# A partial product put off by one chunk, and its bank's copy split in two, in a matrix product with RMS norm

## The chip, the cores and the metric

One core of a Trainium2 chip. The metric is the device time of one execution in microseconds (us); lower is better. Engines: PE is TensorE's matmul, PEld its weight load, DVE is VectorE, ACT is ScalarE, POOL is GpSimd (which here issues most loads), SP is SyncE.

## The reference

```python
a, b = randn(2048, 2048), randn(2048, 2048)      # float32; gamma: randn(2048); eps = 1e-5
x = np.matmul(a, b)
rms = np.sqrt(np.mean(x ** 2, axis=-1, keepdims=True) + eps)
return (gamma * x / rms).astype(np.float32)
```

## The kernel before

Only the head of the kernel, its first 40 us, is touched. There the first four blocks of 128 rows of A are multiplied with the left half of B while both still arrive. The contraction of 2048 is cut into eight chunks `kp` of two contraction tiles `kt` (128 each).

Each chunk is three loads: one slice of A, 4 x 128 rows by 256 columns, and two tiles of B, each 128 x 1024. They are cast from float32 to bf16 on the way.

```python
    def load_head(kp):
        nc.gpsimd.dma_start(
            out=ah(kp),
            in_=a[0:HB * P, kp * W2:(kp + 1) * W2].rearrange("(r p) k -> p r k", p=P))
        load_b(0, kp)                      # two dma_starts, one per contraction tile
```

The slice of A is transposed on TensorE, eight transposes into the one PSUM bank `tbank`, and VectorE copies it out:

```python
    def transpose_head(kp):
        bank = ps_t.tile([P, CH], FP32, name="tbank")        # pool ps_t has one buffer
        ...                                                  # 8 transposes of ah(kp), line 168
        nc.vector.tensor_copy(out=head_at[:, 2 * kp:2 * kp + 2, :, :], in_=view)   # line 173
```

Seven of the eight output groups (4 row blocks x 2 column halves) have a bank of their own and accumulate over all chunks (line 388). The eighth has none. It is computed as a partial product per chunk, also in `tbank` (line 419), and added up in SBUF:

```python
    def stream_in_parts(g, kp):
        part = ps_t.tile([P, CH], FP32, name="tbank")
        for t in range(2):
            nc.tensor.matmul(part, head_at[:, 2 * kp + t, g[0], :], head_rhs(g[1], 2 * kp + t),
                             start=(t == 0), stop=(t == 1))
        x = x_chunk(*g)
        if kp == 0:
            nc.scalar.copy(out=x, in_=part)
        else:
            nc.vector.tensor_tensor(out=x, in0=part, in1=x, op=ALU.add)
    ...
    for kp in range(KP):
        ...                                                  # loads of chunk kp + 4
        before = [lambda: transpose_head(kp + 1)] if kp + 1 < KP else []
        ...
        stream(groups1, kp, before, len(groups1) + (5 if kp == 0 else 3))
        ...
        stream_in_parts(last1, kp)
```

In chunks 0 to 6 `stream` issues the 14 matmuls of the seven groups: the first tile for all groups, then the second. The transposes of the next chunk are put in before the 13th matmul in chunk 0 and before the 11th in chunks 1 to 6.

Of the kernel before, what the change touches and what calls it, by code (L numbers as in the profile page):

```python
# [17 lines left out]
def kernel(  # L18
# [13 lines left out]
    nc = tc.nc  # L32
# [27 lines left out]
    head_at = consts.tile([P, KT, HB, P], BF16, name="head_at")  # L60
# [31 lines left out]
    for h, queue in enumerate((nc.sync, nc.scalar)):  # L92
        queue.dma_start(out=a0f[:, 2 * h:2 * h + 2, :],
                        in_=a[2 * h * P:(2 * h + 2) * P, 0:W2].rearrange("(r p) k -> p r k", p=P))

    def ah(kp):
        return ah_slot[(kp - 1) % NAH]
# [7 lines left out]
# [4 lines that stand above are left out]
        load_b(0, kp)  # L109
# [53 lines left out]
    def transpose_head(kp):  # L163
        bank = ps_t.tile([P, CH], FP32, name="tbank")
        view = bank.bitcast(BF16).rearrange("p (t r m) -> p t r m", t=2, r=HB)
        for t in range(2):
            for r in range(HB):
                nc.tensor.matmul(  # L168
                    view[:, t, r, :], ah(kp)[:, r, t * P:(t + 1) * P], identity,
                    is_transpose=True,  # L170
                    start=(t == 0 and r == 0), stop=(t == 1 and r == HB - 1),
                )
        nc.vector.tensor_copy(out=head_at[:, 2 * kp:2 * kp + 2, :, :], in_=view)  # L173

    a16 = {}

# [77 lines left out]
    def a_sums(g, which, lo=0, hi=KP):  # L254
        a11, a12, a21, a22 = (quarter(g, r, c) for r in range(2) for c in range(2))
        terms = {1: (a11, a22, ALU.add), 2: (a21, a22, ALU.add), 5: (a11, a12, ALU.add),
                 6: (a21, a11, ALU.subtract), 7: (a12, a22, ALU.subtract)}
        for s in which:
            x, y, op = terms[s]
            nc.vector.tensor_tensor(out=sum_of(g, s)[:, lo:hi, :], in0=x[:, lo:hi, :],  # L260
                                    in1=y[:, lo:hi, :], op=op)
# [4 lines left out]
    def b_sums(j, kp):  # L266

        b11, b12, b21, b22 = (b_quarter(j, kp, r, c) for r in range(2) for c in range(2))
        for n, (x, y, op) in enumerate(((b11, b22, ALU.add), (b12, b22, ALU.subtract),
                                        (b21, b11, ALU.subtract))):  # L270
            nc.vector.tensor_tensor(out=sums[j][:, n, kp, :], in0=x, in1=y, op=op)

    def b_sums_in_place(j, kp):

        flat = raw[j][kp].rearrange("p t n -> p (t n)").rearrange("p (q n) -> p q n", q=4)
        nc.vector.tensor_tensor(out=flat[:, 1:3, :], in0=flat[:, 1:3, :], in1=flat[:, 0::3, :],  # L276
                                op=ALU.add)
# [49 lines left out]
    def x_chunk(mb, c):  # L327
        return x_tile(mb, c // 2)[:, (c % 2) * CH:(c % 2 + 1) * CH]
# [55 lines left out]
    def head_rhs(c, kt):  # L384
        return raw[c // 2][kt // 2][:, kt % 2, (c % 2) * CH:(c % 2 + 1) * CH]
# [10 lines left out]
    def load_later(n):  # L396
        for _ in range(min(n, len(later))):
            kind, which = later.pop(0)
            load_b(1, which) if kind == "b" else load_half(HB + which // 2, which % 2)

    def stream(groups, kp, before=(), when=None):


        order = [(g, kt) for kt in (2 * kp, 2 * kp + 1) for g in groups]
        if kp == KP - 1 or (kp == 0 and not before):
            order.sort(key=lambda x: groups.index(x[0]))
        for n, (g, kt) in enumerate(order):
            if n == (when or len(groups)):
                for work in before:
                    work()  # L410
            if kt == 0:
                banks[g] = new_bank()
            head_matmul(banks[g], *g, kt)

    def stream_in_parts(g, kp):

        part = ps_t.tile([P, CH], FP32, name="tbank")
        for t in range(2):
            nc.tensor.matmul(part, head_at[:, 2 * kp + t, g[0], :], head_rhs(g[1], 2 * kp + t),  # L419
                             start=(t == 0), stop=(t == 1))  # L420
        x = x_chunk(*g)
        if kp == 0:
            nc.scalar.copy(out=x, in_=part)
        else:
            nc.vector.tensor_tensor(out=x, in0=part, in1=x, op=ALU.add)

    def evict(groups, on_vector):
        for n, g in enumerate(groups):
            copy = nc.vector.tensor_copy if n in on_vector else nc.scalar.copy
            copy(out=x_chunk(*g), in_=banks[g])  # L430
# [3 lines left out]
    last1 = (HB - 1, 1)  # L434
# [5 lines left out]
    for kp in range(KP):  # L440
        if kp + 4 < KP:
            load_head(kp + 4)
        else:
            load_later(1)
        before = [lambda: transpose_head(kp + 1)] if kp + 1 < KP else []
        if kp in early_sums:
            before.append(lambda: a_sums(PAIR, *early_sums[kp]))
        stream(groups1, kp, before, len(groups1) + (5 if kp == 0 else 3))
        if kp == KP - 1:
            evict(groups1, (1, 3, 5))  # L450
        stream_in_parts(last1, kp)
        if kp > 0:
            b_sums(0, kp - 1)
        if 0 < kp < KP - 2:
            b_sums_in_place(0, kp - 1)
# [400 lines left out]
```

## Time and profile before

| | before |
|---|---|
| time, median of the first three runs | 221.25 us (220.96 to 224.42) |
| span of the profiled run | 219.3 us |
| PE busy | 209.2 us, 95% |
| waits listed for PE | 1.4, 1.0 and 0.4 us, the last ending at 11.44 us |

Read such a profile from the busiest engine: PE has almost nothing to give but its waits. The timeline of PE from the third wait on (columns: start us, duration us, engine, line, operation, names, shapes, count, and in brackets the idle time before and what ended it):

```profile
11.44 0.59 PE L419 MATMUL tbank<-b,head_at 128*128 128x512 bf16 x2 [0.35 <-DVE head_at L173]
11.87 2.32 PE L388 MATMUL acc<-b,head_at 128*128 128x512 bf16 x10
14.02 0.61 PE L168 MATMUL tbank<-identity,early 128*128 128x128 bf16 x8
14.47 1.03 PE L388 MATMUL acc<-b,head_at 128*128 128x512 bf16 x4
15.42 0.59 PE L419 MATMUL tbank<-b,head_at 128*128 128x512 bf16 x2
15.85 2.32 PE L388 MATMUL acc<-b,head_at 128*128 128x512 bf16 x10
```

A row's duration includes the drain of its last matmul, so rows overlap; go by the starts. Chunk 0's partial product starts at 11.44, after 0.35 us of idleness. Chunk 1 runs from 11.87 with the transposes for chunk 2 at 14.02, and chunk 2 begins at 15.85.

### The profile page before, as it was taken

Reading aid. Unit: us, or ns where it says so; the run is one execution under the profiler, and the core shown is the slowest. Engines: PE = TensorE matmul, PEld = TensorE weight load, DVE = VectorE, ACT = ScalarE, POOL = GpSimd, SP = SyncE. Lnnn points to the kernel's source line nnn. Section 1 sums busy time; section 2 is a strip of 40 time slices with the busy share of each in tenths; the row PEclk is TensorE's granted clock in tenths of the full one; section 3 lists DMA queues with packets and bytes.
Section 4 is the critical chain, followed back from the end, with each engine's and each line's share of the span. In section 5 each row is a group of like instructions: output and inputs, shape, how many; then the busy total and the mean of one; then the engine's idle time right before and its main releaser. Section 6 shows DMA issues by size and latency. Waiting matters only on the chain.

```text
span 219.3 us, 3043 instructions
## 1 busy us (share of the span) xinstructions
PE 209.2 (95%) x1032; PEld 97.5 (44%) x1032; DVE 166.0 (76%) x326; ACT 126.9 (58%) x263; POOL 36.4 (17%) x75
## 2 busy tenths in 40 slices
PE   7799999999999999999999999999999999999970
PEld 3344544444455444444444444444444444444440
DVE  1128799999899998989795639846794659787781
ACT  2110002920599898688745997399747996334471
POOL 7554443443020002100200002000200000000040
PEclk9999999999999999999999999999999999999997
DMA  7999999999929698938799049955699249145045
GB/s 152 171 202 206 199 205 209 211 208 221 412 95 341 226 278 208 380 159 234 211 303 400 16 87 269 361 232 96 170 295 396 56 89 365 69 178 208 1 180 204
DMA packets 36864, 46.60 MB, mean 213 GB/s; under 512 B 22256, under 2 KB 26352, under 8 KB 35568
## 3 DMA queue, kind: packets, MB, share of 16 engines
q0 software_dynamic: 10608, 23.86, 44.2%
q1 hardware_dynamic: 25824, 22.02, 33.2%
q10 hardware_dynamic: 416, 0.52, 0.7%
q8 instruction: 8, 0.13, 0.2%
q14 instruction: 8, 0.07, 0.1%
HBM read 34.60 MB, written 16.78 MB: 234 GB/s over the span
## 4 chain that ended last, share of the span: by engine, by line
PE 92%; DMA 3%; issue 1%; ACT 1%; POOL 1%; DVE 0%; ACTq 0%; POOLq 0%
PE acc L285 71%; PE acc L388 16%; DMA early<-in_a_dram 3%; PE tbank L419 2%; PE tbank L168 2%; PE acc L800 1%; POOL b L102 0%; PE tbank L185 0%; PE acc L185 0%; ACT x L739 0%; DVE head_at L173 0%; ACT sq L803 0%; ACT rms L352 0%; POOL t_left masks.py:199 0%; POOL t_left masks.py:197 0%
## 5 line engine op out<-in xcount | busy, mean ns | idle before, releaser
L285 PE MATMUL acc<-b,s 128*128 128x512 bf16 x408 | 93.2, 379 | 0.0
L285 PEld LDWEIGHTS <-s 128*128 128x128 f16 (+1 forms) x512 | 49.9, 98 | 59.9 <-DVE s L260 0.4
L388 PE MATMUL acc<-b,head_at 128*128 128x512 bf16 x176 | 43.0, 379 | 1.1 <-DMA b<-in_b_dram 1.0
L303 ACT ACTIVATE sq<-x 128x512 bf16<-128x512 f32 x53 | 33.4, 630 | 6.9 <-DVE x L732 3.0
L370 DVE SCALAR_TENSOR_TENSOR x<-x,r,gamma_sb 128x1024 f32<-128x1024 f32 x28 | 34.9, 1282 | 0.7
L219 ACT ACTIVATE sq<-a 128x1024 bf16<-128x1024 f32 x24 | 25.3, 1053 | 2.2 <-DMA a<-in_a_dram 1.6
L388 PEld LDWEIGHTS <-head_at 128*128 128x128 bf16 x176 | 16.8, 98 | 20.4 <-issue 1.3
L242 ACT ACTIVATE head_at<-a,s 128x2048 f16<-128x2048 f32 x10 | 20.0, 1998 | 3.4 <-DVE s L229 3.3
L102 POOL DMA_DIRECT2D b<-in_b_dram x32 | 17.2, 541 | 20.5 <-DMA b<-in_b_dram 14.6
L430 ACT COPY x<-acc 128x512 f32<-128x512 f32 x5 | 2.9, 582 | 24.6 <-PE acc L388 24.6
L285 PEld LDWEIGHTS <-head_at 128*128 128x128 f16 (+1 forms) x112 | 10.9, 98 | 13.2
L285 PE MATMUL acc<-early,head_at 128*128 128x512 bf16 x64 | 14.5, 379 | 0.0
L285 PEld LDWEIGHTS <-at_even 128*128 128x128 f16 x96 | 9.4, 98 | 11.3
L285 PE MATMUL acc<-early,s 128*128 128x512 bf16 x56 | 14.2, 379 | 0.0
L260 DVE TENSOR_TENSOR s<-head_at 128x1024 f16<-128x1024 f16 (+5 forms) x22 | 13.4, 636 | 0.1
L616 DVE TENSOR_TENSOR x<-x,x 128x512 f32<-128x512 f32 x9 | 6.2, 693 | 8.8 <-ACT x L614 8.3
L127 POOL COPY pace<-x 128x1 f32<-128x1 f32 x4 | 1.7, 413 | 66.3 <-DVE x L625 65.0
L598 ACT COPY x<-acc 128x512 f32<-128x512 f32 x9 | 5.2, 573 | 11.5 <-PE acc L285 11.5
L285 PE MATMUL acc<-t_left,s 128*128 128x512 bf16 x48 | 11.3, 379 | 0.0
L173 DVE COPY head_at<-tbank 128x1024 bf16<-128x1024 bf16 x7 | 4.8, 692 | 8.5 <-PE tbank L168 8.4
L784 POOL TENSOR_SCALAR x<-x,r 128x512 f32<-128x512 f32 x1 | 2.7, 2653 | 51.2 <-DVE r L346 51.2
L276 DVE TENSOR_TENSOR b<-b 128x1024 bf16<-128x1024 bf16 x16 | 10.8, 689 | 0.2
(113 smaller groups left out, 238.0 us busy)
## 6 DMA issues: line engine op xcount, KB each, us to landing
out_dram<-x SPq DMA_DIRECT2D x29, 512.0 KB, 3.7
a<-in_a_dram POOLq DMA_DIRECT2D x10, 1024.0 KB, 8.8
b<-in_b_dram POOLq DMA_DIRECT2D x32, 256.0 KB, 10.1
a<-in_a_dram POOLq DMA_DIRECT2D x4, 512.0 KB, 9.8
early<-in_a_dram POOLq DMA_DIRECT2D x7, 256.0 KB, 10.1
gamma_sb<-in_gamma_dram POOLq DMA_DIRECT2D x2, 512.0 KB, 8.4
out_dram<-x SPq DMA_DIRECT2D x3, 256.0 KB, 2.6
out_dram<-a SPq DMA_DIRECT2D x1, 512.0 KB, 3.3
```

Source lines behind the costliest of these rows:

```text
L102: nc.gpsimd.dma_start(out=raw[j][kp][:, t, :], in_=b[lo:lo + P, j * HALF:(j + 1) * HALF])
L173: nc.vector.tensor_copy(out=head_at[:, 2 * kp:2 * kp + 2, :, :], in_=view)
L219: nc.scalar.activation(out=junk, in_=a32[mb][:, h * HALF:(h + 1) * HALF], func=ACTF.Square, scale=2.0 ** -8, accum_out=n2[:, h:h + 1])
L242: nc.scalar.activation(out=a16[mb], in_=a32.pop(mb), func=ACTF.Copy, scale=factor.pop(mb))
L260: nc.vector.tensor_tensor(out=sum_of(g, s)[:, lo:hi, :], in0=x[:, lo:hi, :], in1=y[:, lo:hi, :], op=op)
L276: nc.vector.tensor_tensor(out=flat[:, 1:3, :], in0=flat[:, 1:3, :], in1=flat[:, 0::3, :], op=ALU.add)
L285: nc.tensor.matmul(bank, lhsT[:, kp, :], rhs, start=(start and kp == 0), stop=(kp == KP - 1), skip_group_check=not start)
L303: nc.scalar.activation(out=sq[:, 0:CH], in_=src, func=ACTF.Square, scale=inv_sqrt_n, accum_out=msq[mb][:, c:c + 1])
L370: nc.vector.scalar_tensor_tensor(out=x, in0=x, scalar=inverse_of[mb], in1=gamma_sb[:, h * HALF:(h + 1) * HALF], op0=ALU.mult, op1=ALU.mult)
L388: nc.tensor.matmul(bank, head_at[:, kt, r, :], head_rhs(c, kt), start=(kt == 0), stop=(kt == KT - 1))
L598: nc.scalar.copy(out=c, in_=one[1])
L616: nc.vector.tensor_tensor(out=t, in0=t, in1=x12, op=ALU.add)
```

## The change

Chunk 0's partial product has to wait for the copy that empties its bank. The change puts its two matmuls off and joins them to chunk 1's partial product, so that PE can go on with chunk 1 at once. To let chunk 1 start early, the copy that it needs is made in two, one per contraction tile.

```diff
-        nc.vector.tensor_copy(out=head_at[:, 2 * kp:2 * kp + 2, :, :], in_=view)
+        step = 1 if kp == 1 else 2
+        for t in range(0, 2, step):
+            nc.vector.tensor_copy(out=head_at[:, 2 * kp + t:2 * kp + t + step, :, :],
+                                  in_=view[:, t:t + step, :, :])
...
-    def stream_in_parts(g, kp):
+    def stream_in_parts(g, kps):
         part = ps_t.tile([P, CH], FP32, name="tbank")
-        for t in range(2):
-            nc.tensor.matmul(part, head_at[:, 2 * kp + t, g[0], :], head_rhs(g[1], 2 * kp + t),
-                             start=(t == 0), stop=(t == 1))
+        kts = [2 * kp + t for kp in kps for t in range(2)]
+        for kt in kts:
+            nc.tensor.matmul(part, head_at[:, kt, g[0], :], head_rhs(g[1], kt),
+                             start=(kt == kts[0]), stop=(kt == kts[-1]))
         x = x_chunk(*g)
-        if kp == 0:
+        if kts[0] == 0:
             nc.scalar.copy(out=x, in_=part)
...
-        stream_in_parts(last1, kp)
+        if kp > 0:
+            stream_in_parts(last1, (0, 1) if kp == 1 else (kp,))
```

## The prediction

> **What bounds the kernel now.** I read the page first, then the waits of the tensor engine, then the chain of work that ended last, then the timeline of the first 20 us. The page says that the matmul engine is nearly the whole span, and the waits say how little of it is to be had. In the waits, the columns are who waited for whom, us in total, times, longest:
>
> ```profile
> PE 209.2 (95%) x1032; PEld 97.5 (44%) x1032; DVE 166.0 (76%) x326; ACT 126.9 (58%) x263; POOL 36.4 (17%) x75
> ...
> PE acc L147 <- DVE pace L137: 1.4, 1, 1.4
> PE acc L388 <- DMA b<-in_b_dram: 1.0, 1, 1.0
> PE tbank L419 <- DVE head_at L173: 0.4, 1, 0.4
> ```
>
> PE is listed with three waits in 219.3 us. The third, 0.4 us, is the one that the change aims at: the first partial product (L419) writes the one bank "tbank", which holds the transposes until VectorE has copied them out (L173). After that wait nothing at all holds PE up, so every later instruction keeps its distance from it, and whatever the head gains or loses arrives undiminished at the end. The chain of work says what is just ahead of it (start us, us, what):
>
> ```profile
> 3.02 6.97 DMA early<-in_a_dram
> 9.99 0.05 issue
> 10.04 0.63 PE tbank L168 x8
> 10.67 0.02 issue
> 10.69 0.70 DVE head_at L173
> 11.40 0.04 issue
> 11.44 0.59 PE tbank L419 x2
> 12.03 2.16 PE acc L388 x10
> 14.19 0.45 PE tbank L168 x8
> ```
>
> So the head is paced by a load: the slice of A for chunk 1 lands at 9.99. The stretch from 10 to 14 us is what the change rearranges. Now the detail that decides this prediction, from the weight loads (PEld) in the timeline (start us, us, idle before in brackets), where the transposes of the next chunks begin:
>
> ```profile
> 10.03 0.45 PEld L168 LDWEIGHTS <-early 128*128 128x128 bf16 x8 [0.59 <-DMA early<-in_a_dram]
> ...
> 13.88 0.58 PEld L168 LDWEIGHTS <-early 128*128 128x128 bf16 x8 [0.19 <-DMA early<-in_a_dram]
> ...
> 17.87 0.56 PEld L168 LDWEIGHTS <-early 128*128 128x128 bf16 x8 [0.20 <-DMA early<-in_a_dram]
> ...
> 21.77 0.65 PEld L168 LDWEIGHTS <-early 128*128 128x128 bf16 x8
> ```
>
> The transposes of chunk 2 could not load their weights before 13.88, because their slice of A had not landed. PE lost nothing by it: it was still busy with earlier matmuls until 14.02. But there are only 0.13 us between "data there" and "PE free". PE cannot reach those transposes much sooner than it does. The loads themselves do not depend on PE here: they run at some 200 GB/s with all DMA engines busy, and the queue issues the next when an earlier one has landed. The two halves of B for chunk 1 (issued at 3.79 and 4.32) took this long to land, minimum, median and maximum of the two:
>
> ```profile
> DMA to landing us min/median/max: 7.5/7.8/8.2
> ```
>
> Hence 3.79 + 7.5 = 11.3 for its first contraction tile and 4.32 + 8.2 = 12.5 for its second.
>
> **What the Trainium skill says.** (1) "PSUM — Partial Sum Buffer", section "PSUM bank collisions raise a hardware error", has it that two engines may not touch one bank at the same time and that access is to be guarded by bank. That is why the partial product waits for the whole copy (11.44 against the copy's end at 11.38 to 11.40); splitting the copy alone would not free it, and the change therefore takes the partial product away from that place. (2) "VectorE: DVE Perf Modes", section "The TRN2 errata — SBUF-src ops pay a fixed extra latency per instruction", gives a copy out of PSUM as 120 + FD/Accel cycles at 0.96 GHz, so a half does not take half the time. At 2x for bf16 that is 658 ns for 1024 elements, where the trace has 692, so the trace agrees within 5%. (3) "TensorE: Matmul & The Clock Gate", section "Back-to-back issue gap", gives 518 cycles at 2.4 GHz, 216 ns, for 512 columns in isolation, and about 131 ns sustained. The trace bears out the first only: ten matmuls take 2.16 us. (4) "DMA: Bandwidth & Descriptors", section "Anatomy of one DMA — SWDGE (gpsimd) path", says that waits on semaphores happen on the issuing sequencer and not in the DMA engines. The trace agrees: the issuing queue idles "until DMA" again and again, so landings follow one another whatever PE does.
>
> **The change, part by part.** It removes no matmul: two of chunk 0's partial product go from behind chunk 0 to behind chunk 1, at 216 ns each, 0.43 us in both places. It makes one copy of 692 ns into two, and it turns one VectorE add of 693 ns (chunk 1's) into nothing, as one ScalarE copy now serves both chunks. VectorE has room there (3.08 us busy of 4 from 16 to 20 us in the windows view), so only what PE waits for counts.
>
> The half copy has a twin in the kernel, the same cycles at 2x for bf16 as at 1x for f32 (a group of the by-form view; busy us, mean ns, idle):
>
> ```profile
> L161 DVE CAST head_at<-tbank 128x256 bf16<-128x256 f32 x2 | 0.8, 420 | 2.1 <-PE tbank L157 2.1
> ```
>
> Now PE's path, before and after, both from the same landing at 9.99 and the transposes at 10.04:
>
> Before. Partial product at 11.44; two matmuls, 0.43; chunk 1's first matmul at 11.87. Ten matmuls, 2.16, to 14.03 (the trace has the transposes at 14.02; data there at 13.88). Transposes and four matmuls, then the copy is waited for briefly, partial product at 15.42, two matmuls, and chunk 2 begins at 15.85.
>
> After. PE is free at 10.49 + 2 x 0.216 = 10.92. The first half of the copy runs from 10.69 to 10.69 + 0.42 = 11.11, and with 0.04 for the signal chunk 1 could begin at 11.15. But its first tile of B lands at 11.26 to 11.3, and with 0.04 it begins at 11.30. So the wait for the copy becomes a wait for a load, 11.30 - 11.15 = 0.15 longer than intended. This is 11.87 - 11.30 = 0.57 earlier than before, of which 0.43 is only work put off and 0.14 is gained. The second half of the copy ends by 11.5 and the second tile of B lands at 12.5; both are needed at 11.30 + 7 x 0.216 = 12.81, so neither is felt. Ten matmuls end at 11.30 + 2.16 = 13.46. Then the transposes of chunk 2 want their slice of A, and it is there at 13.88. PE stands idle for 0.42. They run at 13.89, only 0.13 earlier than before. The rest of chunk 1 keeps its shape, so its partial product starts at 15.42 - 0.13 = 15.29, and has four matmuls, 0.86, in place of two. Chunk 2 begins at 16.15, against 15.85.
>
> Sum: +0.43 - 0.13 = +0.30 us. Put differently, the two matmuls sat in a stretch that the loads hold open anyway, and cost nothing there; behind chunk 2's transposes they cost their full time. From there on no load catches PE: the next slice of A is usable at 17.87, and PE now comes for it at about 18.30 instead of 18.00. The margin grows with each chunk (usable at 17.87, wanted at 18.00; usable before 21.77, wanted at 21.98). PE is busy in all of the following windows, so the 0.30 goes through to the end: 221.25 + 0.30 = 221.55.
>
> **The rivals.** (A) The author's view: the 0.4 us wait goes and nothing takes its place. If loads were always early, chunk 1 would begin at 11.15, 0.72 sooner, less the 0.43 put off: a gain of 0.29, about 221.0. For it speaks that the list of PE's waits shows this wait and no load after 8.70. Against it speaks the weight-load row at 13.88, which is a load already landing at the last moment; a list of waits shows only what bound, not what stands right behind it. (B) The loads are a little slower in the timed runs than in the profile, so that PE waits for them in later chunks too. Then the 0.43 put off is swallowed in the next wait, and the difference tends to 0, about 221.3. For it speaks that the margins are only 0.13 to 0.2 us in chunks 2 and 3; against, that they grow as PE needs 3.98 us per chunk (transposes at 14.02, 18.00, 21.98 in the timeline) and the loads about 3.9 (the seventh slice of A is issued at 23.47 and takes 9.9: from 9.99 to 33.4 are six chunks of 3.90). (C) The loads come a little earlier after the first slice: each 0.1 us takes 0.1 off the loss, down to the gain of (A). (D) VectorE becomes the bound, since the second copy comes on top: 0.42 x 2 - 0.69 is +0.15 us at a place where it idles, against one add of 0.69 removed later. Nothing in the profile speaks for it; it would make 0.
>
> **Range and chances.** All mechanisms lie between -0.3 and +0.45 us. The three times before are 220.96, 221.25 and 224.42, so the median itself is uncertain by some 0.3, and the run after may meet another mean. I say 221.5, with 220.9 to 222.2 for 8 in 10. Two per cent are 4.4 us, more than ten times any mechanism here: faster 0.01, same 0.98, slower 0.01.
>
> **What would show it right or wrong.** Right: in the profile after, PE's wait for L173 is gone; chunk 1's first matmul starts near 11.30, released by the load of B; PE has a new wait of about 0.4 us before L168 for the load into "early" near 13.5 to 13.9; four matmuls of L419 stand together near 15.3; the last matmul ends about 0.3 later, measured from the landing of the first slice. Two half copies of about 420 ns each. Wrong: the transposes of chunk 2 start before 13.7 measured from the same landing (rival A or C), or PE waits for loads again in chunks 3 to 7 (rival B), or the half copy takes clearly more than 0.42 us.

## The result, and the profile after

| | before | after |
|---|---|---|
| time, median of 6 runs each in the same rounds | 221.22 us (220.85 to 224.42) | 221.36 us (221.16 to 221.46) |
| ratio, 95% interval | | 1.0001 (0.9977 to 1.0025) |

A ratio is the mean time of one kernel's fast runs over that of the other's of the same rounds, so it is not quite the ratio of the medians. Of before, the run of 224.42 is slow and left out of the ratio. The interval is some 0.5 us to either side of nothing, so the timing alone cannot tell a loss of 0.3 us from none. What settles the matter is the traces.

In the changed kernel the lines have moved: 391 is the head's matmul (388 before), 423 the partial product (419), 175 the copy (173). First its busy row and its list of waits of PE (who waited for whom, us in total, times, longest):

```profile
PE 208.5 (95%) x1012; PEld 97.5 (44%) x1032; DVE 165.3 (75%) x326; ACT 126.9 (58%) x263; POOL 36.3 (17%) x75
...
PE acc L391 <- DMA b<-in_b_dram: 0.6, 2, 0.4
PE acc L391 <- DVE head_at L161: 0.4, 1, 0.4
PE tbank L168 <- DMA early<-in_a_dram: 0.3, 1, 0.3
```

(Twenty matmul records are missing from this trace, 1012 instead of 1032; so busy sums of PE aren't compared.) The wait for the copy is gone. In its place are a wait for a tile of B and a new one, L168 for the slice of A. The timeline of PE shows where they are:

```profile
9.76 0.62 PE L168 MATMUL tbank<-identity,early 128*128 128x128 bf16 x8
10.22 0.59 PE L391 MATMUL acc<-b,head_at 128*128 128x512 bf16 x2
11.02 2.32 PE L391 MATMUL acc<-b,head_at 128*128 128x512 bf16 x10 [0.20 <-DMA b<-in_b_dram]
13.61 0.62 PE L168 MATMUL tbank<-identity,early 128*128 128x128 bf16 x8 [0.27 <-DMA early<-in_a_dram]
...
15.01 1.02 PE L423 MATMUL tbank<-b,head_at 128*128 128x512 bf16 x4
15.87 2.32 PE L391 MATMUL acc<-b,head_at 128*128 128x512 bf16 x10
```

At first sight chunk 2 begins when it did before, 15.87 against 15.85. But this trace started luckier. The slice of A for chunk 1 landed at 9.71 instead of 9.99 (3.02 + 6.97 in the chain of the prediction), before anything that was changed. The transposes start 0.04 to 0.05 after that landing in both traces. The chain of work that ended last now comes from another load, the slice of A for chunk 2, which lands at 4.82 + 8.74 = 13.56; before, it came from the slice for chunk 1 (columns: start us, us, what):

```profile
4.82 8.74 DMA early<-in_a_dram
```

To compare traces I measure from the landing of the slice for chunk 1, as the DMA records give it:

- D: from that landing to the first matmul of chunk 2. Before 15.85 - 9.99 = 5.86; after 15.87 - 9.71 = 6.16. That is **0.30 us longer**.
- E: from that landing to the end of the last matmul, the start of its row plus its duration. The last rows of PE, before and after:

```profile
210.30 1.91 PE L800 MATMUL acc<-b,s 128*128 128x256 bf16 x16
```

```profile
210.43 1.91 PE L805 MATMUL acc<-b,s 128*128 128x256 bf16 x16
```

E is 210.30 + 1.91 - 9.99 = 202.22 before and 210.43 + 1.91 - 9.71 = 202.63 after, **0.41 us longer**. So PE fell 0.11 us further back beyond chunk 2. That is in chunk 7, the 14 matmuls of its groups, on PE before and after:

```profile
35.74 3.18 PE L388 MATMUL acc<-b,head_at 128*128 128x512 bf16 x14
```

```profile
35.77 3.29 PE L391 MATMUL acc<-b,head_at 128*128 128x512 bf16 x14
```

The same 14 take 3.29 instead of 3.18 us. The weight loads show where, after the second matmul's had been made and its data was not there:

```profile
35.55 0.31 PEld L391 LDWEIGHTS <-head_at 128*128 128x128 bf16 x2
36.09 0.96 PEld L391 LDWEIGHTS <-head_at 128*128 128x128 bf16 x5 [0.23 <-issue]
```

The second tile of B for chunk 7 landed at 36.05 in this trace, and the second matmul, due at 35.77 + 0.22 = 35.98, began at 36.09. The profile labels the gap only "issue"; I read it as the load because the landing is 0.04 ahead of it. Before, the tile landed at 35.89, and the matmul began on time at 35.96.

The whole balance of the two traces: 0.28 won by the earlier landing, 0.30 lost up to chunk 2, 0.11 lost in chunk 7, which makes +0.13 for the last matmul (212.34 against 212.21).

The 0.41 of E is not a cost of the change, though. From that second matmul to the end both traces take 176.25 us (212.21 - 35.96 and 212.34 - 36.09), so the trace after ended when it did because this tile landed at 36.05. In the rhythm of the kernel before, the matmul comes 35.96 - 9.99 = 25.97 us after the first landing. With the landings of the trace after it would have been due at 9.71 + 25.97 = 35.68 and would have waited for the same tile. By this estimate, which takes the landings as given, the kernel before would have ended at the same time: a late load swallows what was lost ahead of it. (The tiles of B have buffers of their own, so these loads do not wait for PE to free one.) What is compared between the kernels is therefore D; E tells something only where no later load was late.

### The profile page after: what moved, and what is told of

The parts are those of the page before. It is cut to its first block, busy times and chain, and to the rows that moved or that the text cites. A ratio compares the mean times of both kernels' runs of the same rounds, so it can differ in the third digit from the quotient of the medians.

```text
span 219.4 us, 3024 instructions
## 1 busy us (share of the span) xinstructions
PE 208.5 (95%) x1012; PEld 97.5 (44%) x1032; DVE 165.3 (75%) x326; ACT 126.9 (58%) x263; POOL 36.3 (17%) x75
## 4 chain that ended last, share of the span: by engine, by line
PE 90%; DMA 4%; POOL 2%; issue 1%; ACT 1%; DVE 0%; ACTq 0%; POOLq 0%
PE acc L288 71%; PE acc L391 15%; DMA early<-in_a_dram 4%; PE tbank L423 2%; PE tbank L168 1%; POOL b L102 1%; PE acc L805 1%; PE tbank L188 0%; PE acc L188 0%; POOL early L106 0%; ACT x L744 0%; ACT sq L808 0%; ACT rms L355 0%; POOL t_left masks.py:199 0%; POOL t_left masks.py:197 0%
## 5 line engine op out<-in xcount | busy, mean ns | idle before, releaser
L391 PE MATMUL acc<-b,head_at 128*128 128x512 bf16 x171 | 42.2, 379 | 1.2 <-DMA b<-in_b_dram 0.6
L175 DVE COPY head_at<-tbank 128x1024 bf16<-128x1024 bf16 (+1 forms) x8 | 4.9, 624 | 9.8 <-PE tbank L168 9.7
```

The source lines that it names most:

```text
L175: nc.vector.tensor_copy(out=head_at[:, 2 * kp + t:2 * kp + t + step, :, :], in_=view[:, t:t + step, :, :])
L391: nc.tensor.matmul(bank, head_at[:, kt, r, :], head_rhs(c, kt), start=(kt == 0), stop=(kt == KT - 1))
```

## The experiments

My theory: PE waits in chunk 1 for the slice of A of chunk 2, which lands when it lands. Up to that point work is free; the two matmuls were moved from before that point to after it, and cost 0.43 us there. Rivals: the split copy, or the bank, or scatter explains it.

| kernel | landing | D | E | median us | before, same rounds | ratio (95%) |
|---|---|---|---|---|---|---|
| before | 9.99 | 5.86 | 202.22 | 221.22 | | |
| before_again | 10.05 | 5.86 | 202.22 | 221.13 (1 run) | 221.15 | |
| after | 9.71 | 6.16 | 202.63 | 221.36 | 221.22 | 1.0001 (0.9977 to 1.0025) |
| after_again | 10.04 | 6.16 | 202.64 | 221.40 | 221.19 | 1.0006 (0.9985 to 1.0027) |
| split_only | 9.98 | 5.94 | 202.31 | 221.33 | 221.18 | 1.0010 (0.9998 to 1.0022) |
| defer_only | 10.03 | 6.16 | 202.53 | 221.37 | 221.18 | 1.0005 (0.9994 to 1.0017) |
| free_before | 10.03 | 5.86 | 202.23 | 221.14 | 221.18 | 0.9997 (0.9984 to 1.0010) |
| free_after | 10.05 | 5.61 | 201.97 | 220.92 | 221.18 | 1.0003 (0.9984 to 1.0023) |
| gap_fill | 9.50 | 6.35 | 202.71 | 221.61 | 221.19 | 1.0031 (0.9998 to 1.0064) |
| gap_fill_sooner | 10.03 | 6.15 | 202.71 | 221.46 | 221.15 | 1.0003 (0.9968 to 1.0038) |
| early_slot | 9.70 | 5.68 | 202.33 | 221.25 | 221.19 | 1.0001 (0.9981 to 1.0020) |
| early_slot_tail | 9.55 | 5.68 | 202.43 | 220.93 | 221.19 | 0.9993 (0.9971 to 1.0015) |

Landing, D and E are in us. In after, after_again, early_slot and early_slot_tail a later load of the head was late, and in gap_fill_sooner PE was held up near 109 us (both below), so there E is no measure of the edit. Every interval of a ratio holds 1, so none of these kernels can be told from before by its time. D, however, repeats to 0.01 us in the two kernels that were profiled twice. So does E, in after by luck: its late tile landed 26.34 us after the first landing both times.

### split_only: the copy split, the matmuls left where they were

```diff
-        nc.vector.tensor_copy(out=head_at[:, 2 * kp:2 * kp + 2, :, :], in_=view)
+        step = 1 if kp == 1 else 2
+        for t in range(0, 2, step):
+            nc.vector.tensor_copy(...)          # as in the change
```

> Only the copy is split; chunk 0's partial product stays behind chunk 0. Measure D: from the landing of A's slice for chunk 1 to the first matmul of chunk 2 (5.86 us before, 15.85 - 9.99; 6.16 after, 15.87 - 9.71). Theory 1 (the bank is released only when both halves are out, and loads pace the rest): the partial product still waits for the second half, about 0.07 longer than for the one copy (0.76 against 0.69 us), so D is 5.86 to 5.95 and the time is that of before within 0.2 us. Rival (the split alone is what gains): the wait before the partial product falls from 0.35 to some 0.1 us and D to 5.6.

```profile
11.50 0.61 PE L422 MATMUL tbank<-b,head_at 128*128 128x512 bf16 x2 [0.42 <-DVE head_at L175]
```

The partial product waits 0.42 us instead of 0.35, because the bank is free only when both halves are out. D is 5.94, 0.08 more than before, where 0.07 was expected. Alone, the split costs.

### defer_only: the matmuls put off, the copy whole

The changed kernel with the first hunk of the diff taken back.

> Only the two matmuls are put off; the copy stays whole. Theory 1 (PE waits for A's slice of chunk 2 whatever the copy does): chunk 1 begins 0.14 later than with the split, at the end of the whole copy, but the transposes of chunk 2 begin at the same distance of 3.9 us from the landing of chunk 1's slice as after the change, the wait before them is shorter (0.1 to 0.3 us), and D is 6.1 to 6.2 as after the change. Rival (the split is what the change lives on): D is 0.15 to 0.3 longer than after the change, 6.3 to 6.5. Total time within 0.3 us of both kernels either way.

```profile
11.48 2.33 PE L388 MATMUL acc<-b,head_at 128*128 128x512 bf16 x10 [0.35 <-DVE head_at L173]
13.93 0.62 PE L168 MATMUL tbank<-identity,early 128*128 128x128 bf16 x8
...
15.33 1.02 PE L420 MATMUL tbank<-b,head_at 128*128 128x512 bf16 x4
16.19 2.32 PE L388 MATMUL acc<-b,head_at 128*128 128x512 bf16 x10
```

Chunk 1 begins 1.45 us after the landing instead of 1.31 with the split, and yet the transposes start 3.90 after it in both, and D is 6.16 in both. So the split buys nothing in the changed kernel: what it wins is waited away before the transposes. Before the transposes PE stands from 11.48 + 2.16 = 13.64 to 13.93, 0.29 us. Here no tile was late in chunk 7, and E is 202.53, 0.31 above before. A loss at chunk 2 does go through to the end when no later load is late.

### free_before and free_after: the loads taken out of PE's way

Both give a wrong result (relative error 0.68). From chunk 1 on, the transposes read the slice of A of chunk 1 and the matmuls read a tile of B of chunk 0. A seventh slot keeps that slice from being overwritten, and all loads still go out. The same edit was made to both kernels:

```diff
+    NAH = 7
+    ah_slot.append(early[:, 2048:3072].rearrange("p (r k) -> p r k", r=HB))
-                    view[:, t, r, :], ah(kp)[:, r, t * P:(t + 1) * P], identity,
+                    view[:, t, r, :], ah(1)[:, r, t * P:(t + 1) * P], identity,
     def head_rhs(c, kt):
+        if c < 2 and kt >= 2:
+            return raw[0][0][:, 0, 0:CH]
```

> Wrong result on purpose: the kernel before, but from chunk 1 on the first half's matmuls read one tile of B that landed early and the transposes read A's slice of chunk 1, so that PE waits for no load of chunks 1 to 7; all loads are still issued. Theory 1 (in the kernel before PE itself paces chunk 1 on): D is as before, 5.85 to 5.9, and the time is within 0.15 us of before. Rival (loads already cost the kernel before something): D or the time falls by over 0.2 us.

> Wrong result on purpose: the changed kernel with the same loads taken out of PE's way. Theory 1 (the load took the place of the copy's wait): now the change gains what was intended: chunk 1 begins 0.15 us after its copy can allow, the 0.3 to 0.4 us wait before the transposes of chunk 2 is gone, D is 5.55 to 5.65, which is 0.5 to 0.6 shorter than after the change (6.16) and 0.28 shorter than with the loads freed and without the change; the time is 0.2 to 0.35 us below that kernel's. Rival (the 0.43 us put off is lost for another reason than the loads): D stays at 6.1 to 6.2.

(In the second text, "0.15 us after its copy can allow" is a slip; meant was as soon as its copy allows, 0.15 earlier than the load had allowed.) PE of free_after:

```profile
13.40 0.61 PE L170 MATMUL tbank<-identity,early 128*128 128x128 bf16 x8
...
14.80 1.02 PE L427 MATMUL tbank<-b,head_at 128*128 128x512 bf16 x4
15.66 2.32 PE L395 MATMUL acc<-b,head_at 128*128 128x512 bf16 x10
```

Without the loads, the kernel before keeps its D of 5.86: its PE was not held by them. The changed kernel's D falls from 6.16 to 5.61, and its transposes start 3.35 us after the landing instead of 3.90. Then the change gains about what it was meant to: 0.25 in D and 0.26 in E (201.97 against 202.23). The medians differ by 0.22 us in the same sense. Two stragglers (222.32 and 221.55) among six runs of free_after keep the ratio from showing it, so this rests on the traces, one of each kernel. This is the clearest of the experiments: the same change, worth +0.30 in D with the loads and -0.25 without them. It frees the slices of A and the tiles of B at once; that the slice is the one that counts is seen from defer_only, where chunk 1 began 0.14 later and the transposes did not.

### gap_fill and gap_fill_sooner: two more matmuls where PE stood idle

To the changed kernel, two matmuls of 512 columns are added (0.43 us, result unused): in gap_fill just before the transposes of chunk 2, in gap_fill_sooner two matmuls earlier.

```diff
+    def idle_matmuls():
+        spare_bank = ps_t.tile([P, CH], FP32, name="tbank")
+        for kt in range(2):
+            nc.tensor.matmul(spare_bank, head_at[:, kt, 0, :], head_rhs(0, kt),
+                             start=(kt == 0), stop=(kt == 1))
+        if kp == 1:
+            before.insert(0, idle_matmuls)      # gap_fill; in _sooner: called at n == 8 in stream
```

> The changed kernel with two more matmuls of 512 columns (0.43 us of PE's work, their result unused) put just before the transposes of chunk 2, where PE stood idle after the change. Theory 1 (that stretch is held open by the load of A's slice, which does not depend on PE): they are free or nearly so; the transposes of chunk 2 start at 3.85 to 3.95 us after the landing of chunk 1's slice as after the change, the 0.27 us wait before them shrinks to at most 0.05, D is 6.15 to 6.25, and the time is that of the changed kernel within 0.15 us. Rival (PE's work counts wherever it stands): D is 6.55 to 6.6 and the time 0.4 us above the changed kernel's.

```profile
12.95 0.60 PE L434 MATMUL tbank<-b,head_at 128*128 128x512 bf16 x2
13.60 0.61 PE L168 MATMUL tbank<-identity,early 128*128 128x128 bf16 x8
```

This missed: D is 6.35, not 6.15 to 6.25. The transposes start at 13.60, just after the added row's end at 13.55, and not at the slice's landing at 13.32. They go to the same bank, so I took it that they wait until the second added matmul has drained. That would be a wait of the experiment's own making, so I ran it again with the pair placed earlier.

> As gap_fill, where the transposes of chunk 2 began 4.10 us after the landing of chunk 1's slice and not 3.9: they wrote the same bank as the two added matmuls and began 0.05 us after the second of these had ended, a wait that the experiment itself had made. Here the two added matmuls (0.43 us of work, result unused) stand two matmuls earlier, so that their end lies behind two others. Theory 1 (the stretch is held open by the load): transposes 3.85 to 3.95 us after that landing, D 6.15 to 6.2 as after the change, i.e. the added work is free. Rival (PE's work counts there): transposes at 4.3 or later, D 6.55 to 6.6.

```profile
13.06 0.59 PE L436 MATMUL tbank<-b,head_at 128*128 128x512 bf16 x2
...
13.93 0.61 PE L168 MATMUL tbank<-identity,early 128*128 128x128 bf16 x8
```

Now the transposes start 3.90 after the landing and D is 6.15. So 0.43 us of further work cost nothing in that place, while the same amount put behind the transposes had cost 0.43. The stretch is held open by the load. E is 202.71 here, 0.18 more than in defer_only with nearly the same D. The trace shows why, far behind the head: a later block of A landed at 92.87, where after_again has 91.02, and ScalarE waited 3.36 us for it instead of 1.39. So its copy that empties a PSUM bank (line 611 here, 603 in the changed kernel) ended only at 108.92, against 107.07. PE's next matmul into that bank began at 108.96, which is 0.41 after the one before it instead of 0.22. Nothing in the trace ties that landing to the added pair; with one trace I take it for scatter.

### early_slot and early_slot_tail: the put-off work into the open stretch

If that stretch is free, chunk 0's partial product belongs into it. From the kernel before, with the split copy:

```diff
         for n, (g, kt) in enumerate(order):
+            if n == 2 and kp == 1:
+                stream_in_parts(last1, 0)
...
-        stream_in_parts(last1, kp)
+        if kp > 0:
+            stream_in_parts(last1, kp)
```

early_slot_tail also swaps the second and third matmul of chunk 7 (`order[1], order[2] = order[2], order[1]`), so that its second tile of B is wanted later.

> The split copy is kept, but chunk 0's partial product is put behind the first two matmuls of chunk 1, into the stretch held open by the loads, with its own ScalarE copy. Theory 1: chunk 1 begins when its tile of B is there (1.3 us after the landing of its slice of A), the two matmuls fill the idle time, the transposes of chunk 2 start 3.85 to 3.95 us after that landing, and D is 5.70 to 5.78, against 5.86 before and 6.16 after: a gain of about 0.1 us on the kernel before. Since PE then reaches chunk 7 earlier than that chunk's second tile of B lands in some runs, part of it may be lost there; time 220.95 to 221.25. Rival (the bank cannot be had that early, as the ScalarE copy of the partial product holds the transposes up): D stays at or above 5.86 and PE waits for ScalarE before the transposes.

> As early_slot, and in chunk 7 the second and third matmul are swapped, so that its second tile of B is wanted 0.22 us later. If that tile is what takes back small gains of the head (in the trace after the change PE stood 0.11 us before that matmul), there is no gap in PE's matmuls of chunk 7 here, D is as in early_slot, and the last matmul ends 0 to 0.15 us earlier than in early_slot relative to the landing of A's slice for chunk 1. Rival (no load binds there): no difference to early_slot. Time 220.9 to 221.2.

PE of early_slot:

```profile
11.38 0.59 PE L424 MATMUL tbank<-b,head_at 128*128 128x512 bf16 x2
11.81 1.89 PE L391 MATMUL acc<-b,head_at 128*128 128x512 bf16 x8
13.54 0.62 PE L168 MATMUL tbank<-identity,early 128*128 128x128 bf16 x8
...
15.38 2.32 PE L391 MATMUL acc<-b,head_at 128*128 128x512 bf16 x10
17.81 0.62 PE L168 MATMUL tbank<-identity,early 128*128 128x128 bf16 x8
```

D falls to 5.68, below the kernel before by 0.18, which beats what I expected (5.70 to 5.78). Some 0.06 of that is the loads': the first tile of B for chunk 1 landed 1.21 us after the slice of A in both traces (10.91 - 9.70 and 10.76 - 9.55), and 1.27 before (11.26 - 9.99). But the gain doesn't last. Ten matmuls from 15.38 end at 15.38 + 2.16 = 17.54, and the transposes of chunk 3 start at 17.81: their slice landed at 17.76. In early_slot_tail the same befell chunk 5, whose slice landed at 25.67 with the transposes at 25.72. E is 202.33 and 202.43, which is 0.1 and 0.2 more than before.

That is not a loss of the edit's. The first landing came 0.29 and 0.44 us earlier than in the trace before, but the slices that PE then waited for hardly did (17.76 and 25.67, against 17.83 and 25.69 before). In the rhythm of the kernel before, the transposes of chunk 3 start 18.00 - 9.99 = 8.01 us after the first landing and those of chunk 5 25.96 - 9.99 = 15.97. With these landings that is 17.71 and 25.52, so they would have waited too, 0.10 and 0.20 us, and E would have been some 202.32 and 202.42: an estimate, but the measured figures within 0.01. The late slice swallowed the whole gain, as the late tile of B swallowed the loss in the trace after. What was expected of early_slot_tail, an end 0 to 0.15 earlier than in early_slot by E, missed for the same reason: another slice was late. The median of early_slot_tail, 220.93, is the lowest of all kernels with a correct result, but its interval holds 1, and its trace explains no gain. So I do not call it faster. The swap in chunk 7 did work in its one trace. The second tile of B landed at 35.87 there, and in the old order the second matmul would have wanted it at 35.51 + 0.22 = 35.73. With the swap the third matmul wants it at 35.94, and all 14 run without a gap. In early_slot the tile was in time (35.64, wanted at 35.55 + 0.22 = 35.77).

### after_again and before_again: scatter

The two kernels once more, unchanged.

> The changed kernel once more, for its scatter: D is 6.1 to 6.2 again, with the slice of A for chunk 1 landing near 10.0 us rather than 9.71 as in the first trace (10.0 in five other traces); the last matmul then ends about 0.3 us later than before, near 212.5 us, unless chunk 7's tile of B lands so late that it sets the end. Time 221.2 to 221.6. Rival (the change moves the loads and makes them land earlier): the slice lands at 9.7 again.

> The kernel before once more, for the scatter of its trace: D is 5.86 within 0.03 whatever the landing of A's slice for chunk 1 (9.5 to 10.05 us in the ten traces so far), and the last matmul ends 202.2 to 202.3 us after that landing (202.63 and 202.64 in the two traces after the change), if no load binds in chunks 3 to 7. Rival (D and the end follow the loads even before the change): D differs by over 0.1.

D and E come out as in the first traces: 6.16 and 202.64; 5.86 and 202.22. In after_again too, chunk 7's tile was late (36.38), and its second matmul began at 36.42 where 36.09 + 0.22 = 36.31 was due. That is the exception named in the expectation; the last matmul ended at 212.68 and not near 212.5. The early landing of the first trace after, 9.71, was not the change's doing: here it is 10.04. In the twelve traces this landing lies anywhere from 9.50 to 10.05. The time follows it: the profiled executions of before, after, after_again and before_again took 221.06, 221.16, 221.47 and 221.13 us, and their last matmuls ended at 212.21, 212.34, 212.68 and 212.27. The differences are 8.8 to 8.9 us throughout. A profiled time is thus the landing, plus E, plus some 8.8. The landing's scatter of 0.55 us is larger than anything the change does.

## Why the prediction was right or wrong

**Right: the class, the time, and the mechanism up to chunk 2.** 221.36 us lies in the range of 220.9 to 222.2, near the 221.5 named. That alone decides nothing, for the figure of every rival (221.0 to 221.3) lies in that range too; it is D that tells them apart.

- *The wait for the copy becomes a wait for a tile of B.* Chunk 1 was to begin 1.31 us after the landing (11.30 - 9.99); it began at 1.31, and in free_after, where no load is in the way, at 1.19.
- *The half copy takes 0.42 us.* The two together took 0.76 us in the timeline, 420 ns each by the group view.
- *PE then stands idle before the transposes of chunk 2.* Predicted was 0.42 us, from the end of the last matmul's turn. In the trace the last of the ten matmuls started at 12.96 and its turn ended at 13.17, so 0.43 until 13.61. The list of waits says 0.27, as it counts from the end of the drain. defer_only, free_after and gap_fill_sooner show that the load is what holds this place.
- *D grows by 0.30: 0.43 put off, 0.13 gained.* Measured 0.30 in both traces of the changed kernel and in defer_only.

Rival A, the gain that the change was made for, exists: it is -0.25 in free_after, where 0.29 was reckoned. The load takes it. Rival C, loads that come earlier after the first slice, did not occur: the slice for chunk 2 landed 3.85 us after that for chunk 1 in both first traces (13.84 - 9.99 and 13.56 - 9.71). Rival D, VectorE as the bound, fell: in the waits of the changed kernel, the only ones of PE for VectorE are those of the warm-up and of chunk 0's first copies (L161).

**Wrong: one step.** "From there on no load catches PE" and "The margin grows with each chunk". The lines shown gave 14.02 - 13.88 = 0.14 for chunk 2 and 18.00 - 17.87 = 0.13 for chunk 3, which is no growth yet. I had read the margin from the slices of A and not looked at the tiles of B of chunk 7, whose order of matmuls wants the second tile at once. There the margin before was 35.96 - 35.89 - 0.04 = 0.03 us. In both traces of the changed kernel that tile was late, and its landing, not the 0.30, set the end: E grew by 0.41 and 0.42. Rival B had this right, that a later wait for a load swallows what was put off, so that the difference tends to 0; it is what the estimate above gives for these two traces. The sign named for it, PE waiting for loads again in chunks 3 to 7, did appear. It looked to the small margins of chunks 2 and 3, though; the one that gave way was chunk 7's. In defer_only that tile was not late, and the 0.30 arrived as predicted. Whether a tile is late depends on the run: it landed 25.90 and 25.78 us after the first slice before, and 26.34 in both traces after. Two traces each are too few to say that the change makes it later, and in defer_only, with the same work put off, it was 25.76.

A smaller slip: 658 ns for the copy is an estimate from the formula that the prediction cites, and 692 is 5.2% above it, not within 5%. No term of the sum rests on it.

**Size of the whole.** Predicted was +0.30; the medians differ by 0.14 and 0.21 us in the two sets of rounds. By the account above, 0.30 arrives in a run in which no later load is late and nothing in one where a load is late enough, so 0.14 and 0.21 would fit, but the timed intervals of some 0.5 us to either side admit all of these. A landing that scatters by 0.55 us hides an effect of this size in any case; how the landings fell in the unprofiled runs cannot be seen.

## What to carry to other kernels

A wait at the top of an engine's list can lie inside a longer one that is not listed: before removing it, ask what the engine will meet next and when that arrives, for instance from weight loads that already wait for data although the matmuls lose nothing. Work that stands in a stretch held open by a load is free there, and costs its full time once it is moved behind the load's arrival. A load that is late further on swallows gains and losses alike, so neither can be read at the end of such a trace. For effects smaller than a run's scatter, compare traces from a common event such as a landing: here that made D agree to 0.01 us in two traces of one kernel where the times differed by up to 0.3.

## What the Trainium skill lacked or had wrong

- "TensorE: Matmul & The Clock Gate", section "Back-to-back issue gap": it gives about 131 ns per 512-column matmul as the sustained figure in a stream and calls 216 ns the isolated gap. In every trace here the stream of weight loads and matmuls runs at 216 ns (ten starts in 2.16 us).
- "DMA: Bandwidth & Descriptors", section "Bandwidth": it has no figure for loads that cast. It gives some 358 GB/s as a core's share of HBM when both cores of a pair stream, and 425 GB/s for 16 MB loaded by a single core. A tile of B is 128 x 1024 float32 in HBM, 0.524 MB, and landed 1.24 us after the one before it (11.26 to 12.50), which is 423 GB/s read. Over six chunks of 3.90 us, with three loads of 0.524 MB each, it is 403 GB/s. Both are estimates from landings, and both lie between these two figures. The profile counts the bf16 side, about 203 GB/s.
- No page that I read has the scatter of a kernel's first loads: the same load landed between 9.50 and 10.05 us in twelve traces, and later loads did not always shift with it.
